# One store split in three so that one of 16 DMA engines carries 16 KB less: an RMSNorm kernel at the DMA limit

## The chip, the cores and the metric

One core of a Trainium2 chip. The metric is the device time of one execution in microseconds (us). A run of the kernel before has a median of 162.84 us (three runs, 162.62 to 162.89).

## The reference

```python
x: float32 [16, 1024, 512];  gamma: float32 [512];  eps = 1e-5
rms = np.sqrt(np.mean(x ** 2, axis=-1, keepdims=True) + eps)
return np.maximum(x / rms * gamma, 0).astype(np.float32)
```

16,384 rows of 2 KB are read once and written once: 33.6 MB each way.

## The kernel before

The rows are cut into eight chunks of 4 MB. In a chunk, each of 128 partitions holds 16 consecutive rows, so its part is one contiguous run of 32 KB on both sides. Six slots in SBUF take the chunks in turn. SyncE issues every load and store of them; ScalarE makes the sums of squares and the square root, VectorE the rest, in place. GpSimd only passes on that a load has landed.

```python
K = 16; G = 8; nslots = 6                      # nchunks = 8
xv = x2.rearrange("(c p k) d -> c p k d", p=P, k=K)
ov = out2.rearrange("(c p k) d -> c p k d", p=P, k=K)

def store(i):
    nc.sync.dma_start(out=ov[i], in_=slot_ap(i)).then_inc(sem_slot[i % nslots], 16)

for i in range(nchunks):                       # SyncE
    nc.sync.wait_ge(done, per * (i + 1))       # VectorE has finished chunk i
    store(i)
    if i >= 1 and nxt < nchunks:
        nc.sync.wait_ge(sem_slot[nxt % nslots], 32)
        ...                                    # load chunk nxt into the slot that came free
# ... ScalarE's and VectorE's loops ...
with nc.sync.register("landed") as landed:     # the end: every store has landed
    nc.sync.reg_mov(landed, 32)
    for s in range(nchunks - nslots, nslots):
        nc.sync.wait_ge(sem_slot[s], landed)
    nc.sync.reg_mov(landed, 64)
    for s in range(nchunks - nslots):
        nc.sync.wait_ge(sem_slot[s], landed)
```

The last chunk (number 7) lies in slot 1, and the last wait of the program is for that slot.

## Time and profile before

| | kernel before |
|---|---|
| time, median of three runs | 162.84 us |
| time of the profiled execution; span of its instructions | 162.69 us; 160.9 us |
| share of 16 DMA engines' span filled by the main queue's packets | 97.6% |
| VectorE, ScalarE busy | 126.0, 86.3 us |
| last store issued; its first packet; its last confirmation | 146.46; 148.68; 159.88 us |

The times are from the recorded results; span, share and busy times are from the profile's page. The last row is from the timeline and from the trace's records of DMA packets and of semaphore increments. The last store's sixteen increments come from 158.72 to 159.88 us, and SyncE's next instruction after the wait for them starts at 159.89: the slowest of the engines ends the wait, so at the end the spread among engines counts, not their mean. The lines that carry this are in the prediction.

### The profile page before, as it was taken

The numbers are of one execution on the slowest core, as the hardware profiler recorded it, in microseconds if no ns is written. First come the engines' busy times: TensorE is split into PE (matmuls) and PEld (weight loads), VectorE is DVE, ScalarE is ACT, GpSimd is POOL, SyncE is SP. The second block draws the span as 40 slices with busy tenths as digits, with TensorE's granted clock in tenths as the row PEclk, the third lists the DMA queues.
The fourth block names the chain that finished last, engine by engine and source line by source line (L and its number), as shares of the span: only waits on it lengthen the run. The fifth ranks groups of instructions, "written<-read, shape, count | busy, mean of one in ns | idle before, by whom it ended". The sixth has DMA issues, their size and how long they took to land. (4 is left out here: it accounts for less than half of the span.)

```text
span 160.9 us, 1006 instructions
## 1 busy us (share of the span) xinstructions
DVE 126.0 (78%) x164; ACT 86.3 (54%) x273; POOL 0.2 (0%) x4
## 2 busy tenths in 40 slices
DVE  1103989898989899999999999999999999994000
ACT  3088929889988988988900198503994000000000
POOL 0000000000000000000000000000000000000000
DMA  5999999999999998999999999999999999999993
GB/s 155 434 432 415 521 391 391 513 399 391 489 424 391 481 432 367 415 391 489 424 391 489 424 391 448 464 391 440 456 407 432 456 415 424 464 415 424 464 407 138
DMA packets 2456, 67.12 MB, mean 417 GB/s; under 512 B 276, under 2 KB 276, under 8 KB 280
## 3 DMA queue, kind: packets, MB, share of 16 engines
q1 hardware_dynamic: 2448, 67.11, 97.6%
q10 hardware_dynamic: 8, 0.01, 0.0%
HBM read 33.56 MB, written 33.55 MB: 417 GB/s over the span
## 5 line engine op out<-in xcount | busy, mean ns | idle before, releaser
L124 ACT ACTIVATE junk<-slots 128x512 f32 x128 | 74.5, 582 | 30.6 <-ACTq L120 30.3
L148 DVE SCALAR_TENSOR_TENSOR slots<-slots,rstd,gamma_sb 128x512 f32 x128 | 86.2, 747 | 4.8 <-DVEq L145 4.8
L155 DVE TENSOR_SCALAR slots<-slots x16 | 36.7, 2294 | 2.4 <-DVEq L154 0.2
L124 ACT ACTIVATION_READ_ACCUMULATOR junk<-slots x128 | 23.9, 187 | 0.0
L142 DVE RECIPROCAL rstd<-rms x16 | 3.1, 196 | 6.3 <-DVEq L138 6.3
L131 ACT ACTIVATE rms<-ss,eps_sb x16 | 4.8, 301 | 3.0 <-ACTq L130 3.0
L135 DVE LOAD_MASK_SELECT gamma_sb<-gseed x1 | 0.0, 14 | 5.8 <-DMA gseed<-in_gamma_dram 5.8
L116 ACT ACT_TABLE_LOAD x1 | 1.3, 1283 | 2.8 <-issue 2.8
L109 DVE MEMSET gseed<- 128x512 f32 x1 | 0.5, 485 | 1.1 <-SPq L90 1.1
L135 DVE STREAM_SHUFFLE gamma_sb<-gseed 128x512 f32<-128x512 f32 x1 | 0.7, 715 | 0.0
L180 POOL MEMSET const-bfloat16-1.0<- 128x1 bf16 x1 | 0.1, 103 | 0.0
L180 POOL MEMSET const-uint8-127<- 128x1 uint8 x1 | 0.1, 102 | 0.0
L180 POOL MEMSET const-float32-0.0<- 128x1 f32 x1 | 0.1, 100 | 0.2 <-issue 0.2
L180 POOL MEMSET const-float32-1.0<- 128x1 f32 x1 | 0.1, 99 | 0.0
L110 DVE MEMSET eps_sb<- 128x1 f32 x1 | 0.1, 59 | 0.0
## 6 DMA issues: line engine op xcount, KB each, us to landing
out_dram<-slots SPq DMA_DIRECT2D x8, 4096.0 KB, 31.3
slots<-in_x_dram SPq DMA_DIRECT2D x7, 4096.0 KB, 30.3
slots<-in_x_dram SPq DMA_DIRECT2D x2, 2048.0 KB, 9.6
gseed<-in_gamma_dram ACTq DMA_DIRECT2D x1, 8.0 KB
```

What stands on the lines that cost most here:

```text
L109: nc.vector.memset(gseed, 0.0).then_inc(sem_z, 1)
L110: nc.vector.memset(eps_sb, eps).then_inc(sem_z, 1)
L116: nc.scalar.preload_act_table(ACTF.Sqrt)
L124: a = nc.scalar.activation(out=junk[:, j, :], in_=slots[:, bass.ds(base + j * d, d)], func=ACTF.Square, accum_out=ss[:, bass.ds(col + j, 1)])
L131: nc.scalar.activation(out=rms[:, bass.ds(col, G)], in_=ss[:, bass.ds(col, G)], func=ACTF.Sqrt, bias=eps_sb, scale=inv_d).then_inc(sq, 1)
L135: nc.vector.stream_shuffle(gamma_sb, gseed, [0] * 32)
L142: nc.vector.reciprocal(out=rstd[:, bass.ds(col, G)], in_=rms[:, bass.ds(col, G)]).then_inc(sv, 1)
L148: r = nc.vector.scalar_tensor_tensor(out=row, in0=row, scalar=rstd[:, bass.ds(col + j, 1)], in1=gamma_sb, op0=ALU.mult, op1=ALU.mult)
L155: nc.vector.tensor_scalar_max(out=blk, in0=blk, scalar1=0.0).then_inc(done, 1)
L180: nc = _bacc.Bacc("TRN2", target_bir_lowering=False, num_devices=1)
```

## The change

The intent is to take work off one DMA engine that is thought to finish last. The last store is cut so that one row of 2 KB per partition, sent apart by 120 and then by 8 partitions, goes by fifteen of the sixteen engines only.

```diff
+    parts = [(0, P, 0, K)]
+    tail = [(0, P, 0, K - 1), (0, 120, K - 1, K), (120, P, K - 1, K)]
+
     def store(i):
-        nc.sync.dma_start(out=ov[i], in_=slot_ap(i)).then_inc(sem_slot[i % nslots], 16)
+        for p0, p1, k0, k1 in (tail if i == nchunks - 1 else parts):
+            nc.sync.dma_start(out=ov[i][p0:p1, k0:k1, :],
+                              in_=slot_ap(i)[p0:p1, k0:k1, :]
+                              ).then_inc(sem_slot[i % nslots], 16)
 ...
-        nc.sync.reg_mov(landed, 64)
         for s in range(nchunks - nslots):
+            last = tail if s == nchunks - nslots - 1 else parts
+            nc.sync.reg_mov(landed, 48 + 16 * len(last))
             nc.sync.wait_ge(sem_slot[s], landed)
```

Engine numbers are names here; the trace has none. Engine n is the one that a DMA on n + 1 partitions reaches and one on n doesn't; 15 is the one that the 120 partitions miss.

## The prediction

Its sum is 162.84 us less 0.38 to 0.47, so 162.37 to 162.46, put at 162.4 and set at 162.5. One term was to take some of the gain back: a rival in which the small pieces collide (0.1 to 0.2 us in part, 162.55 to 162.65; in full 0.64 us, about 163.0). The smaller lag (162.55 to 162.75) is there for the 162.5, and the rival of another late engine for the upper end of the range, 163.0. The landings of the loads: in the trace the sixteen of a load spread over 0.31 to 0.64 us, the last 0.03 us or less behind the next.

> **What bounds the kernel now.** I read three views in this order: the page's slices and DMA queue lines (which resource is full), the waits of the queue that issues the DMAs (what the program waits for at the end), and the timeline with the stretches of the last 20 us (what still runs there).
>
> The page of the kernel before:
>
> ```profile
> DVE  1103989898989899999999999999999999994000
> ACT  3088929889988988988900198503994000000000
> POOL 0000000000000000000000000000000000000000
> DMA  5999999999999998999999999999999999999993
> ...
> q1 hardware_dynamic: 2448, 67.11, 97.6%
> ```
>
> The DMA row is full from the second slice to the last but one: one queue moves 67.11 MB and its packets fill 97.6% of 16 engines' span. VectorE stops three slices before the end. The chain that the page prints for "what ended last" stops at VectorE's last instruction and so hides the end; the issuing queue's own waits show it:
>
> ```profile
> SPq L87 <- DVE slots L155: 105.2, 6, 26.5
> SPq L75 <- DMA out_dram<-slots: 33.0, 2, 24.2
> SPq L163 <- DMA out_dram<-slots: 12.4, 1, 12.4
> ```
>
> The third line is the end of the program: one wait of 12.4 us for the last store's landing. The timeline shows when that store was issued:
>
> ```profile
> 144.14 2.29 DVE L155 TENSOR_SCALAR slots<-slots  x1
> 146.46 0.33 SPq L87 DMA_DIRECT2D out_dram<-slots  x1
> ```
>
> and the stretches show what runs after it (columns: stretch, its us, busy time of VectorE, ScalarE and GpSimd with their instructions, clock, DMA share, GB/s):
>
> ```profile
> 140.00:150.00 10.00, 6.28 (x8) 0.00 (x0) 0.00 (x0) 1.00 0.99 429
> 150.00:159.90 9.90, 0.00 (x0) 0.00 (x0) 0.00 (x0) 1.00 0.84 361
> 159.90:160.90 1.00, 0.00 (x0) 0.00 (x0) 0.00 (x0) 1.00 0.00 0
> ```
>
> From 150.0 us on only DMA works; 159.90 to 160.90 is the closing handshake, which the change doesn't touch. The store is issued at 146.46, but the engines still drain the store before it: in the packet records the last store's first packet starts at 148.68. So there are 2.2 us of slack between issue and use.
>
> **The last store, engine by engine.** The records don't number the DMA engines, but each engine's packets follow each other without a gap, so 16 chains can be told apart. A 32 KB packet (one partition's 16 rows) took 1213 ns, a 16 KB one 611 ns, a 2 KB one 84 ns and a 4-byte semaphore write 9 ns. A straight line fits all four: 9 ns + 0.0367 ns per byte (27 GB/s for one engine). Starts follow each other 4 ns closer than the durations, so the pitch is 5 ns + 0.0367 ns/B: 1209 ns for 32 KB, 1134 for 30 KB, 80 for 2 KB, 5 for a semaphore write.
>
> The last store's semaphore is raised once by each engine. The sixteen landings run from 158.72 to 159.37 for fifteen engines and 159.88 for the last, which is 0.51 us behind the next. The program waits for the sixteenth. The same single engine lags in the stores before: last against last but one 140.44 to 140.01, then 150.21 to 149.70. In the loads [...]none lags. So this is a straggler that grows over the stores (some of its packets took 1227 to 1246 ns) and enters the last store already 0.37 us late (its first packet starts at 149.71, the next-latest engine's at 149.35). Its final semaphore write is also confirmed more slowly, 0.49 us after it starts, against about 0.35 for the others.
>
> [...]large stores have 16 landings, and the 4-partition gamma load has four packets on four chains and four late increments after an early one. [...]The trace does show one straggler, but not its number. None of the four chains that carry the gamma load[...] is a late one. [...]the pieces here are 2 KB, and the gamma packets, also 2 KB, took 84 ns, as the straight line has it.
>
> **The change part by part.** It doesn't touch the first seven stores, the loads or the arithmetic.
> 1. The first of three stores sends 30 KB for each partition. Each engine: 8 x 1134 + 5 = 9.08 us instead of 8 x 1209 + 5 = 9.68 us. Removed: 0.60 us on all 16.
> 2. The second sends 2 KB for each of 120 partitions, eight pieces on engines 0 to 14: 8 x 80 + 5 = 0.65 us. Net for engines 8 to 14: +0.04 us, for 15: -0.60 us.
> 3. The third sends the last eight 2 KB pieces, one on each of engines 0 to 7: 80 + 5 = 0.09 us. Net for 0 to 7: +0.13 us.
> 4. Two more issues on SyncE. One store's issue took 0.33 us here (0.73 the longest), so the third is out by about 147.3 us, at the latest by 148.7; its descriptors are first needed when the 30 KB part ends, near 157.8. Cost on the path: none.
> 5. The final waits are per slot. The extra register moves come before the last wait and cost nothing; slot 0's store landed at 150.21. The last one now waits for 96 instead of 64.
>
> If the straggler is engine 15, its landing moves from 159.88 to 159.28. The new last one is one of the pair that landed at 159.36 and 159.37, plus 0.04 or 0.13: 159.41 to 159.50. Gain: 0.38 to 0.47 us, not 0.60, because the next-late engines take over. From 162.84 that makes 162.37 to 162.46.
>
> **Rivals.**
> - *The straggler is not engine 15.* If it is among 8 to 14 the end moves by +0.04, if it is engine 7 by +0.13: 162.9 to 163.0. For: the trace doesn't number engines[...]. Against: the change picks 15, which its author must have taken from somewhere. I give this 15%.
> - [...]
> - *The lag is a thing of one execution.* It depends on slow packets spread over 90 us of stores. Another execution can have a smaller lag; then the gain is 0.1 to 0.3 us and the end is set by the other fifteen: 162.55 to 162.75.
> - *Splitting costs fixed time.* If each further DMA added a whole completion on the path (0.35 to 0.5 us each as seen at the end), the time would rise by up to 0.6 us. Against: between the last two stores the packet records show a pitch of 5 ns from a semaphore write to the next data packet, so completions overlap with the next DMA's data.
>
> **Range and chances.** The clean sum gives 162.4; [...]a smaller lag takes some of it back. I set 162.5. The three runs before spread over 0.27 us, and other rivals end near 163.0, so the range is 162.15 to 163.0. Two per cent is 3.3 us. No part of this change can save that: even removing the whole spread among engines (159.88 to 158.72) would be 1.2 us. A loss of 3.3 us would need the 256 KB of small pieces to run at about a sixth of their rate, which I give 1%.
>
> **What would show it right or wrong.** The changed trace should hold 128 fewer packets of 32 KB than before, 128 more of 30 KB, 128 more of 2 KB, and 23 more semaphore writes (15 + 8). The wait at the end should have its last increment near 159.4 to 159.5 with the sixteen engines' ends within 0.8 us, and no lone last one. The straggler right: one chain lacks the 2 KB packets and ends at 159.3 or earlier. [...]The wrong engine: the lone last landing stays, 0.05 to 0.13 later, and the chain without small packets ends about 0.6 us before the others. The SP issues wrong: a gap between 30 KB and 2 KB packets. The prediction is wrong if the time lies outside the range, or if the gain comes with the lone straggler still last.

## The result, and the profile after

The changed kernel takes 163.04 us (median of six runs, 162.82 to 163.41); the kernel before, with the runs of the same rounds, 162.80 us. The ratio is 1.0017, with a 95% interval of 1.0001 to 1.0032: slower by some 0.28 us. A ratio here is the mean time of one kernel's fast runs over that of the other's in the same rounds, so not quite the ratio of the medians quoted; in the experiments below it comes out as recorded when the profiled execution is left out. The time lies 0.04 us above the predicted range, and the sign of the change is the opposite of the predicted one.

The page after, the same lines as before:

```profile
DVE  1103989898989898999999999999999999993000
ACT  3088929889988988988900198503994000000000
POOL 0000000000000000000000000000000000000000
DMA  5999999999999999999999999999999999999992
...
q1 hardware_dynamic: 2599, 67.11, 97.4%
```

The same bytes in 151 more packets: 128 for the row sent apart and 23 more semaphore writes, as predicted. The timeline of the end of the changed kernel, and its stretches (same columns as in the prediction):

```profile
144.23 2.29 DVE L163 TENSOR_SCALAR slots<-slots  x1
146.55 2.08 SPq L93 DMA_DIRECT2D out_dram<-slots  x3
```

```profile
140.00:150.00 10.00, 6.37 (x8) 0.00 (x0) 0.00 (x0) 1.00 0.99 426
150.00:159.90 9.90, 0.00 (x0) 0.00 (x0) 0.00 (x0) 1.00 0.87 371
159.90:161.40 1.50, 0.00 (x0) 0.00 (x0) 0.00 (x0) 1.00 0.00 0
```

The three issues took 2.08 us and were over at 148.63, nine microseconds before the second store's first packet. In the last stretch no DMA engine is busy any more, yet it is 1.50 us long instead of 1.00: the packets end at 159.87, and the store's last confirmation arrives at 160.44. The waits of the issuing queue in the changed kernel, from 140 us on:

```profile
SPq L203 <- DMA out_dram<-slots: 9.9, 1, 9.9
SPq L171 <- DMA out_dram<-slots: 1.2, 1, 1.2
```

The one wait of 12.4 us appears as 1.2 for the store before (it landed at 150.54) and 9.9 for the last. The closing handshake after it is the same 1.0 us.

The packet records hold the answer. I told the chains of the sixteen engines apart as in the prediction. Times are in us; "first" is the start of an engine's first packet of the last store, "last" that of its last semaphore write, "confirmed" the arrival of that write's increment (the trace doesn't say which engine an increment came from: writes and increments are paired in order of time):

| kernel, engine | packets of its last store | first | last | from first to last | confirmed |
|---|---|---|---|---|---|
| before, latest | 8 of 32 KB | 149.71 | 159.39 | 9.68 | 159.88 |
| after, latest | 8 of 30 KB, 8 + 1 of 2 KB | 150.05 | 159.86 | 9.81 | 160.44 |
| after, the one without 2 KB packets | 8 of 30 KB | 149.71 | 158.78 | 9.07 | |

The third line is engine 15, the one that the 120 partitions miss. It was relieved by 0.60 us, exactly as worked out, and it had been the second-latest at the start of the store (149.71 against 150.05 for the latest). But the latest engine is another. It carries a packet of the third store, so it is one of engines 0 to 7: it was burdened, by 0.14 us, where it should have been relieved.

That the profiled executions differ by more (159.88 to 160.44) is mostly not the change's doing: the late engine came into the last store 0.34 us later in this execution. Then 0.14 us are its packets, and 0.09 us its last confirmation, which arrived 0.58 us after the write started instead of 0.49. The last two make 0.23 us, against 0.24 between the medians and 0.28 from the ratio.

### The profile page after: what moved, and what is told of

The parts are those of the page before. It is cut to its first block, busy times and chain, and to the rows that moved or that the text cites. A ratio compares the mean times of both kernels' runs of the same rounds, so it can differ in the third digit from the quotient of the medians.

```text
span 161.4 us, 1008 instructions
## 1 busy us (share of the span) xinstructions
DVE 126.0 (78%) x164; ACT 86.3 (53%) x273; POOL 0.2 (0%) x4
## 3 DMA queue, kind: packets, MB, share of 16 engines
q1 hardware_dynamic: 2599, 67.11, 97.4%
```

## The experiments

Theory: one of engines 0 to 7 is lastingly the late one, and the change adds work to it. Rivals: engine 15 is the late one after all and the splitting costs more than it saves; no engine is lastingly late; each further DMA has a fixed cost. Runs ran on four chips. The profile after leaves engines 0 to 7 open; my first guess among them was engine 7, which no trace had shown. All results were correct.

### Which engine is late: numbering

To number the chains I let ScalarE, idle after 125 us, issue tiny loads of k partitions each with its own packet size, after all arithmetic. In the second numbering of the kernel before, ScalarE's queue has 52 packets: 8 of gamma, as without tags, and 44 for the 22 partitions of the tags, so a data packet and a semaphore write for each partition. The tags found on a chain place it among the engines as named above.

```diff
+    tag_ks = [8, 7, 15, 14, 4, 2, 1, 12]        # second numbering: [7, 6, 5, 4]
+        nc.scalar.wait_ge(done, ngroups)
+        for k in tag_ks:
+            nc.scalar.dma_start(out=tags[0:k, 32 * (k - 1):32 * (k - 1) + 16 + k],
+                                in_=x2[0:k, 0:16 + k]).then_inc(tagged, 16)
```

> Kernel before plus eight tiny loads of 8, 7, 15, 14, 4, 2, 1 and 12 partitions, each of its own size, issued by ScalarE after the arithmetic[...]. Theory 'the straggler is engine 7': the last chain carries the tags 8, 12, 14, 15 and not 7. Rival 'engine 15': the last chain carries no tag at all. Rival 'it differs from run to run': any other. Time within 0.5 us of the kernel before.

163.29 us. The latest chain, confirmed at 160.42 where the next is at 159.30 and earlier, carries the tags of 7, 12, 14 and 15 partitions and not that of 4: it is one of engines 4 to 6. Engine 15 falls, and so does my guess of engine 7: the chain with the tag of 8 but not of 7 ends with the early ones, at 158.4. Had I taken the guess for granted, the numbers so far would have fitted it.

> As the first numbering run with tags of 7, 6, 5 and 4 partitions alone. The first one put the late chain among engines 4 to 6 (it carried the tag of 7 partitions and not that of 4). Theory 'one fixed engine is late': the last chain carries 7 and perhaps 6 and 5, never 4. Rival 'another engine in each execution': anything else, a chain without tags or with all four.

> The changed kernel with the same four tags. Theory 'one fixed engine': the last chain has the same set of tags as in the numbered kernel before, and in its last store it has the packets of all three DMAs; the chain without any 2 KB packet (engine 15) is not last. Rival: the last chain is another one.

163.06 and 163.32 us. In both, the latest chain carries the tags of 7, 6 and 5 partitions and not of 4: engine 4. It is confirmed at 160.25 (the next at 159.27) in the kernel before, and at 160.56 in the changed one, where its last store is 8 packets of 30 KB and nine of 2 KB. The issues of the second of these runs (KB each; the tags have 0.3 to 0.6 KB) show what its packets come from:

```profile
out_dram<-slots SPq DMA_DIRECT2D x1, 3840.0 KB
out_dram<-slots SPq DMA_DIRECT2D x1, 240.0 KB
...
tags<-in_x_dram ACTq DMA_DIRECT2D x1, 0.4 KB
out_dram<-slots SPq DMA_DIRECT2D x1, 16.0 KB
```

The 16 KB store is the one that reaches engine 4 and misses engine 15. So on two chips, and on a third in the two runs with GpSimd below, the latest engine of a numbered profile is engine 4 or, in the first, one of 4 to 6. Five numbered profiles of five, and it is confirmed 0.32 to 1.12 us after the next engine.

### How much room the others have

One more 16 KB packet behind the last store on each of the first k engines; first as a load into a free slot, then as a store to an unused buffer.

```diff
+        nc.sync.wait_ge(sem_slot[3], 32)
+        nc.sync.dma_start(out=slot_ap(3)[0:k, 0:8, :], in_=xv[0][0:k, 0:8, :]).then_inc(extra, 16)
+        # store form: out=aside[0:k, 0:8, :], in_=slot_ap(3)[0:k, 0:8, :]; its wait comes last
```

> Kernel before plus one 16 KB load packet behind the last store on each of engines 0 to 6 (7 partitions), 0.61 us each. Theory 'engine 7 alone is last by about 0.4 us, engine 15 next, 0 to 6 earlier by some 0.7 us': the time rises by 0 to 0.15 us. Rival 'there is no lasting straggler in unprofiled runs' or 'one of 0 to 6 is as late': it rises by about 0.5 to 0.6 us.

> The same with 8 partitions, so engine 7 gets the 16 KB packet too. Theory 'engine 7 is last': the time rises by about 0.6 us over the kernel before, 0.4 to 0.6 us over the probe of 7. Rival 'engine 15 is last': it rises as little as the probe of 7, 0 to 0.15 us.

164.41 and 164.26 us; ratios 1.0090 (1.0073 to 1.0107) and 1.0084 (1.0068 to 1.0101). Both rise alike, by 1.4 us, which is what neither theory expected in size. The likeness fits the numbering, since seven engines already include engine 4. The size is partly my own: I had put the wait for the extra load ahead of the other final waits, which then took 0.3 us in turn, and three of the seven packets took 745 to 980 ns instead of 611.

> Kernel before plus one 16 KB store packet (to an unused buffer in HBM) behind the last store on each of engines 0 to 3, 0.61 us each, its wait placed last. Theory 'the straggler is one of engines 4 to 6, in timed runs as in the profiled ones, about 0.5 us behind': these four have that much room, time rises by 0 to 0.2 us. Rival 'no lasting straggler': it rises by 0.5 to 0.7 us.

> The same on engines 0 to 6, so that the straggler gets the 16 KB packet too. Theory 'the straggler is one of 4 to 6': the time rises by 0.6 to 0.7 us, 0.4 to 0.6 us more than with four. Rival: both probes rise alike.

163.05 us and 163.65 us; ratios 1.0021 (1.0008 to 1.0035) and 1.0038 (1.0024 to 1.0052). Four engines cost less than seven, by 0.28 us from the ratios and 0.6 from the medians. The direction is the theory's, but the intervals overlap, and four cost 0.34 us where I had expected at most 0.2. The packet records show why the second was off: the four extra packets took 734, 1014, 1231 and 1351 ns, and in a packet's 611 ns they would have ended before engine 4. The destination was new; what slowed them is not shown.

### Splitting without shifting, and the change again

> The changed kernel as it is, beside the other three on one chip. Every theory: 0.1 to 0.4 us slower than before (first comparison: 0.28). Theory 'the late engine carries all three parts': its chain in the last store holds eight 30 KB packets, nine 2 KB packets and three semaphore writes, and ends last.

163.05 us, ratio 1.0017 (1.0003 to 1.0030): the result repeats on another chip. The profile is a warning about single profiles. It fell on the slowest of the five runs (163.61 us, not in the ratio), and there the latest chain, confirmed at 160.84, holds eight 2 KB packets, so it is one of engines 8 to 14. The chain with nine that I had expected last is second, at 160.48. So engine 4 is not the last in every execution.

```diff
-    tail = [(0, P, 0, K - 1), (0, 120, K - 1, K), (120, P, K - 1, K)]
+    tail = [(0, 15 * d), (15 * d, 15 * d + d // 2), (15 * d + d // 2, 16 * d)]   # of every partition's 16 * d
```

> The last store in three DMAs that all run on 16 engines: 30 KB, then 1 KB, then 1 KB for each partition. No engine is relieved; each gets 16 packets instead of 8 and two more semaphore writes. Theory 'two more DMAs cost only their packets': +0.09 us, at most 0.2 with a slower final confirmation. Rival 'a fixed cost for each further DMA': +0.5 us or more.

162.81 us, ratio 1.0005 (0.9991 to 1.0018). The issues of this kernel show three stores, all of 128 partitions:

```profile
out_dram<-slots SPq DMA_DIRECT2D x7, 4096.0 KB, 33.7
...
out_dram<-slots SPq DMA_DIRECT2D x1, 3840.0 KB, 12.1
out_dram<-slots SPq DMA_DIRECT2D x2, 128.0 KB, 12.3
```

Three stores cost 0.08 us, about the sum of their packets (per engine 8 x 1134 + 16 x 43 + 15 = 9.77 us against 9.68), and the interval excludes half a microsecond. Here a further DMA behind others on the same queue has no fixed cost of that size. What the change loses is not the splitting as such.

### Taking the late engine's bytes

To relieve a middle engine one needs a DMA that leaves it out. Of the tags, those of 7, 6 and 5 partitions reached engine 4 and that of 4 did not. That 119 partitions go by seven engines and 124 by four, as the next two expectations have it, is an estimate from the semaphore writes of the stores seen: 128 partitions on 16 engines, 120 on 15, 8 on 8 and, in `e8_third_by_four`, 4 on 4 (its packets come to 2599 with 15 + 4 + 4 further writes).

```diff
+    c = 192   # e8: c = 128, pieces (0, 124), (124, P)
+    tail = [(0, P, 0, K * d - c)] + [(a, b, K * d - c, K * d) for a, b in [(0, 119), (119, 126), (126, P)]]
```

> The last 768 bytes of each partition's 32 KB are stored apart, by 119, 7 and 2 partitions, so all of it goes by engines 0 to 6: these get 18 or 19 packets of 33 ns (0.6 us) for 0.23 us taken from each engine. Theory 'engine 7 is last': the last store of engines 7 to 15 ends 0.22 us earlier, of 0 to 6 0.37 us later; 0.1 to 0.25 us faster than before. Rival 'one of 0 to 6 is as late': 0.3 us slower. Rival 'each further DMA has a fixed cost of some tenths on the path': slower by 0.3 us or more.

163.49 us, ratio 1.0035 (1.0019 to 1.0050): 0.57 us slower. This was built on the guess of engine 7 and by that estimate puts all the small pieces on engines 0 to 6, so on engine 4 too. The rival in the expectation, "one of 0 to 6 is as late", fits; the other rival there, a fixed cost for each DMA, forecast the same, and only the even split above speaks against it. By the packet pitch these engines then have 0.38 us more (8 x 1181 + 18 x 33 + 15 = 10.06 us against 9.68). The latest chain's last confirmation came 0.61 us after its write.

> The last 512 bytes of each partition go by 124 and 4 partitions, so by engines 0 to 3 alone: all others have 0.15 us less, these four 0.6 us more. Theory 'engine 4 is late by 0.5 to 0.9 us': between 0.15 us faster and 0.05 us slower than before, the four taking over the end. Rival 'the late engine is among 0 to 3 or none is lastingly late': 0.5 us slower or more.

162.78 us, ratio 1.0003 (0.9987 to 1.0019). In its profile no engine is alone at the end any more: the last increments are at 159.75, 159.82 and 159.83, where before one stood 0.51 us behind. But the four that took the bytes are now as late, so there is no gain to measure. It is the fastest of the split forms by its median, and still no faster than the kernel before. The runs don't show a version that beats it. What the run does show is where there is room: engines 0 to 3 had 0.6 us more each by the packet pitch, and the rival's 0.5 us or more lies outside the interval, which ends at 0.31 us. In `e4_relief7`, with one DMA more, only 0.38 us more on engines 0 to 6 (the estimate above) cost 0.57 us. The two intervals touch at 1.0019 alone (each against the kernel before on its own chip), so of all timed pairs this one says most clearly that the late engine is one of 4 to 6.

GpSimd's queue was tried as another way to leave out one engine; that its second DMA starts where the first stopped was my assumption, not shown by any run (in the diff, numbers stand for names; the tags of 5 and 4 partitions, in both twins, are left out):

```diff
+        nc.gpsimd.dma_start(out=seed[0:5, :], in_=x2[0:5, 0:16]).then_inc(primed, 16)   # first twin only
+        nc.gpsimd.wait_ge(done, ngroups)
+        nc.gpsimd.dma_start(out=ov[7][0:120, 15:16, :], in_=slot_ap(7)[0:120, 15:16, :]).then_inc(row15, 16)
-    tail = [(0, P, 0, K - 1), (0, 120, K - 1, K), (120, P, K - 1, K)]
+    tail = [(0, P, 0, K - 1), (120, 124, K - 1, K), (124, P, K - 1, K)]
```

> The last row of 120 partitions is stored by GpSimd's queue, after a first DMA of 5 partitions on that queue; the last 8 partitions go as two stores of 4 partitions (engines 0 to 3). [...]The tags of 5 and 4 partitions mark engine 4 in the trace. Theory 'engine 4 is the late one': if its chain lacks the 2 KB packets, 0.3 to 0.5 us faster than the changed kernel, 0.1 to 0.3 faster than before. Rival: no faster than the changed kernel. If its chain has them, the run tells nothing of it.

> The same without the first DMA of 5 partitions[...]. Theory 'engine 4 is the late one': like the changed kernel, 0 to 0.4 us slower than before, and slower than the twin by 0.3 to 0.5. Rival 'engine 15': faster than the twin.

163.16 us, ratio 1.0019 (1.0006 to 1.0033), and 162.86 us, ratio 1.0006 (0.9992 to 1.0020). The queue lines of the first twin, then of the second:

```profile
q0 software_dynamic: 112, 0.25, 0.4%
```

```profile
q0 software_dynamic: 80, 0.25, 0.4%
```

In both, fifteen chains carry 4 KB packets of that queue and one carries four packets of 8 bytes in their place; the chain with the tag of 5 but not of 4 carries data in both and is the latest in both (confirmed at 160.40 and 160.01). With the 5-partition DMA first or without it, the second used engine 4. So the condition in the expectation, a late chain without this row, failed, engine 4 was not relieved, and the twins tell nothing of relief. What they add is the number of the late engine on a third chip. Why the first is slower than the second is open.

### Undoing the late engine's share

```diff
-    tail = [(0, P, 0, K - 1), (0, 120, K - 1, K), (120, P, K - 1, K)]
+    tail = [(0, P, 0, K - 1), (0, 120, K - 1, K), (120, 124, K - 1, K), (124, P, K - 1, K)]
```

> The changed kernel with its last 8 partitions sent as two stores of 4 (engines 0 to 3) instead of one of 8 (engines 0 to 7), so that engine 4 has the 30 KB and the eight 2 KB packets only. Theory 'the late engine 4 carried +0.13 us of packets and about 0.1 us of a confirmation that waits for the one before': 0 to 0.1 us slower than before instead of 0.28, though there is one DMA more. Rival 'the number of DMAs or the small packets cost it': still 0.25 us or more slower.

163.00 us, ratio 1.0010 (0.9997 to 1.0023). That is 0.16 us over before, with one DMA more than the changed kernel has, whose ratio was 1.0017. The direction is the theory's, the size is above what I expected, and the interval holds both. The profile shows the small part cleanly: the latest chain has eight 2 KB packets, not nine, and its last confirmation came 0.49 us after its write (159.65 to 160.14), as before the change, not 0.58.

> Changed kernel with four rows (8 KB) of each partition taken out of the first store instead of one: engine 15 has 64 KB less (2.4 us), engines 0 to 7 one 8 KB packet more (0.31 us). Theory 'engine 4 is late': +0.30 to 0.45 us over before. Rival 'engine 15 is late': 0.1 to 0.4 us faster than before, the next-late engines taking over.

> The same with the last 8 partitions sent as 4 and 4: engines 0 to 3 have two 8 KB packets more (0.61 us, about their room), engine 4 none. Theory 'engine 4 is late, 0 to 3 have 0.5 to 0.8 us of room': 0 to 0.2 us over before, 0.2 to 0.4 us under the twin. Rival 'the cost is the number of DMAs': as slow as the twin or slower.

163.18 us, ratio 1.0020 (1.0006 to 1.0035), and 163.26 us, ratio 1.0035 (1.0020 to 1.0049). The first speaks against engine 15: it has 64 KB less, 2.4 us of its work, and the kernel is 0.33 us slower. But this is not decisive, as slow packets on other engines could hide a gain (below). The second missed: sending the last 8 partitions by engines 0 to 3 should have been 0.2 to 0.4 us faster than its twin, and was 0.24 slower by the ratios, with intervals that overlap. The packets tell what I had left out. The 8 KB packets should take 309 ns; in the twins 29 and 26 of 128 took over 1.2 times that, up to 716 and 640. So the pair differs by more than the share of engine 4 and does not measure it. In both profiles another engine, slowed on these packets, is the last: in the first twin the chain that came latest into the last store (149.66) runs through it regularly and makes its last semaphore write at 159.69, the other at 160.04. In the changed kernel all 128 packets of 2 KB took 84 to 92 ns.

### What makes an engine late

```diff
+        nc.vector.wait_ge(sem_slot[3], 32)
+        for j in range(14):                      # on rows of the free slot 3
+            nc.vector.scalar_tensor_tensor(out=row, in0=row, scalar=rstd[:, 0:1], in1=gamma_sb, op0=ALU.mult, op1=ALU.mult)
```

> The kernel before with 14 more VectorE multiplications on a free slot during the last store (about 9.5 us). Theory 'VectorE's work slows the late engine's packets': its 32 KB packets in the last store, all 1213 ns before, are 1218 to 1275 ns in part, and its lag over the next grows by 0.1 us or more in that store. Rival: all stay at 1213.

> The same with 14 ScalarE squares (about 8 us) in place of VectorE's work. Theory 'ScalarE's work slows it': slow packets in the last store. Rival: all stay at 1213 ns. ScalarE stops at 125 us in the kernel before, and slow packets were still seen to 149, so little is expected.

163.06 and 163.16 us, one look each. VectorE worked through the last store, as the timeline of the first shows:

```profile
146.36 9.36 DVE L160 SCALAR_TENSOR_TENSOR slots<-slots,rstd,gamma_sb 128x512 f32<-128x512 f32 x14
146.47 0.33 SPq L87 DMA_DIRECT2D out_dram<-slots  x1
```

From 149.2 us on the kernel before and the changed one have no large packet more than 3 ns over its regular time. With VectorE at work there are four, 2 to 14 ns over; with ScalarE four, 3 to 28 ns over. Together that is 31 and 43 ns, too little to make 0.5 us of lag. But all eight lie on the chain that ends last: each starts where a packet of that chain ends.

That is so before the last store too. In the kernel before, the excess of all engines' packets together is 490 ns from 102 to 112 us, where loads and stores last run side by side, 200 in the next ten and about 70 in each of the three after that. From 112 to 150 us 25 packets are more than 2 ns over, by 411 ns in all, and every one lies on the late chain. That is about its lag of 0.37 us at the start of the last store. All 20 profiles have this: 19 to 26 such packets, 331 to 459 ns in all, on one chain (in five of them it has to be followed across one or two starts that come 7 to 10 ns early). In the numbered profiles it is the chain of engine 4, or of one of 4 to 6. In `e7_after_again` it is the one with nine 2 KB packets; the engine that ended after it had lost 0.57 and 0.59 us on two packets near 102 and 110 us.

So the lag is one engine's own slow packets. In the numbered kernel before, the last confirmation of a store is 0.13 us behind the next at 101.6 us, 0.37 at 111.3, 0.70 at 131.0 and 0.92 at 150.5. Why the packets of this one engine are slow stays open.

## Why the prediction was wrong, point by point

- **What bounds the end: right.** From 150 us on only the last store runs, and the sixteenth confirmation ends it. SyncE's issues were hidden with room to spare.
- **The cost per packet: right.** Engine 15's part fell from 9.68 to 9.07 us (worked out: 9.68 to 9.08), and that of engines 0 to 7 rose by 0.14 us on the latest (worked out: 0.13).
- **"If the straggler is engine 15": this step failed.** I gave it 85%, on the ground that the change's author must have taken the number from somewhere. The trace before did not number the late chain. The first rival, "the straggler is not engine 15", had the right sign and 162.9 to 163.0 us; it named engine 7 and 8 to 14, and numbering shows engine 4. Engine 15 was second-latest at the start of the last store in the profile after, but only fourth to sixth in three others (`e8_third_by_four`, `e7_after_again`, `e5_number_after`).
- **A term was left out of that rival's sum.** Two confirmations close together on the late engine: its last two semaphore writes, 0.086 us apart in the changed kernel, were confirmed 0.19 us apart (160.26 and 160.44). In the first numbering run two writes 5 ns apart were confirmed 0.19 us apart as well. With one 2 KB packet between them, the third store costs the late engine 0.09 us beyond its packet. 162.80 plus 0.14 plus 0.09 makes 163.03, against 163.04 measured. The second term repeats: the engine with the slow packets was confirmed 0.57 to 0.58 us after the last of two such writes in three profiles of the changed kernel, and 0.48 to 0.49 us after a single one in eight others (0.33 to 0.37 us on the other engines in the kernel before). The sum as a whole rests on one profile of each kernel; that this is all of the loss is not shown, as undoing the third store's share moved the ratio only from 1.0017 to 1.0010.
- **Colliding small pieces: wrong for this change.** No 2 KB packet was slow: all took 84 to 92 ns. Slow packets do appear at 8 KB (29 and 26 of 128 in the `e10` twins) and at 16 KB (734 to 1351 ns for the four in `e6_store_probe4`); their cause is not shown.
- **A fixed cost for each DMA: rightly set aside.** The even split cost 0.08 us.
- **The lag differs between executions: right, and larger than I allowed for.** The late engine entered the last store at 149.71 and 150.05 us in the two profiles, and in some runs another engine was last (`e7_after_again` and both `e10` runs).
- **The range was too narrow at the top:** it took the rival's upper value, 163.0, as its end.

## What to carry to other kernels

Before taking work off "the slow engine", number it in the trace: a few tiny DMAs on different counts of partitions place it (here 7, 6, 5 and 4, once a first set had narrowed it to three engines), and an author's choice is not evidence for this kernel. At the end of this program, which is full of DMA, only the last engine's confirmation counted (159.88 us, the next at 159.37), and what relieved another engine by 0.60 us added 0.14 us of packets to the late one. A gain that depends on 0.5 us of lag in one profile needs several profiles first, because the lag itself moves by as much (0.13 to 0.92 us over the stores of one numbered profile).
